# Other SBUF places for the moving operands of a two-layer diffusion backbone, and a DMA scratch of 1 KB

## The chip, the cores and the metric

The kernel runs on one core of a Trainium2 chip. The metric is the device time of one execution in microseconds (us). Before the change the median of three runs is 2012.92 us (2012.64 to 2014.09).

## The reference

Two layers run over 256 latent tokens `x` and 256 context tokens `ctx`, each of width 1024, with the same weights for both. All of it is float32. Cut to what matters:

```python
for l in range(DEPTH):                                   # DEPTH = 2
    m, mc = silu(c) @ w_ada[l] + b_ada[l], silu(c_ctx) @ w_ada[l] + b_ada[l]     # 9 x 1024 each
    x  = x  + 0.5 * m[2]  * swiglu(modulate(rms_norm(x),  m[0],  m[1]),  w1[l,0], w3[l,0], w2[l,0])
    xc = xc + 0.5 * mc[2] * swiglu(modulate(rms_norm(xc), mc[0], mc[1]), w1[l,0], w3[l,0], w2[l,0])
    h, hc = modulate(rms_norm(x), m[3], m[4]), modulate(rms_norm(xc), mc[3], mc[4])
    y, yc = token_mixer(h, hc, w_in[l], ...)             # yc only in layer 0
    x = x + m[5] * y
    x = x + 0.5 * m[8] * swiglu(modulate(rms_norm(x), m[6], m[7]), w1[l,1], w3[l,1], w2[l,1])
    # layer 0 alone: xc likewise
return rms_norm(x, final_g)
def swiglu(h, w1, w3, w2): return (silu(h @ w1) * (h @ w3)) @ w2      # 1024 -> 2816 -> 1024
def token_mixer(h, hc, w_in, ...):
    p = h @ w_in              # one projection: Fourier, retention, attention, gate logits
    f, r, d = fourier(p), retention(p, hc @ w_in), attention(p, hc @ w_in)
    return (g0 * (f @ w_branch_f) + g1 * (r @ w_branch_r) + g2 * (d @ w_branch_d)) @ w_out
```

## The kernel before

Activations stand transposed, channels on the 128 partitions and tokens along the free axis: 512 columns while both streams live, and 256 in the second half of layer 1, where only the latent tokens are left. Every large product is made of three float32r matmuls per 128x128 block of weights (`mm3`, L276 to L282): the weight is cut into a high part `whi` (a cast by ScalarE, L285) and a rest `wlo` (VectorE or, for a few, GpSimd, L286), the activation into `hi` and `lo` in the same manner, and L280, L281 and L282 add whi·hi, whi·lo and wlo·hi in PSUM. TensorE thus loads a new 128x128 weight tile before each matmul, and the activation is the moving operand that streams past it.

Weights come by DMA in pieces of [128, 4, 256] float32 into `wraw` (pool `wr`, four buffers), and the cut pieces stand in `whi` and `wlo` (pool `wh`, four buffers). The last quarter of each `to_residual` has its weights in the pool of its stage instead (tags "a", "b", "c" or "v").

The stages follow one another, named after layer and half: f00 (`ffn(0, 0)`, 512 columns), m0 (`mixer(0)`, 512), f01 and f10 (512), m1 (`mixer(1)`, 256 but for a few products over all 512 tokens), f11 (256). In an FFN the products into `p1`, `p3` read `hhi_f..`/`hlo_f..` (made by `Norm.parts`, L340), and the products into `py` read `ghi`/`glo` (the gated hidden units). In a mixer the products into `pj` (projections) and `pg` (gates) read `hhi_m..`/`hlo_m..`, those into `pb` (branches) `bh`/`bl`, and those into `py` (output) `mhi`/`mlo`. Two products of a mixer (`proj_tok`, L800) work the other way round: there a slice of `hhi_m..` is loaded as the weight, and 384 columns of `whi`/`wlo` move. At the seams between stages (`handover`, L456) the last products of one stage and the first of the next run for 256 columns at a time, and the first products of f11 read `xh`/`xl`, 258 columns wide.

Attention and retention are generators woven with the projections and gates (`weave`, L238), so that TensorE has products to run while VectorE and ScalarE work on masks and softmax. The order on each engine is fixed when the program is built.

Where a tile lies is set by the order in which the pools and their tiles are opened: each pool lays its tiles one after another at the next free byte of a partition. `hhi` and `hlo` have one place each in the pool `hp` for the whole kernel (L331 to L333); the tiles of an FFN lie in a pool opened at L578, those of a mixer in the pools opened at L722, L727, L728 and L1074. A pool named `shift` with one tile of 32 bytes stands ahead of them (L92).

The lines of the products:

```python
def mm3(o, wt, k, c0, x, start, stop):
    hi, lo = wt
    xh, xl = x
    a, b = hi[:, k, c0:c0 + P], lo[:, k, c0:c0 + P]
    te.matmul(o, a, xh, start=start, stop=False)
    te.matmul(o, a, xl, start=False, stop=False)
    te.matmul(o, b, xh, start=False, stop=stop)
```

Of the kernel before, what the change touches and what calls it, by code (L numbers as in the profile page):

```python
# [11 lines left out]
F32 = mybir.dt.float32  # L12
F32R = mybir.dt.float32r
# [4 lines left out]
P = 128  # L18
D = 1024
KD = D // P  # L20
L = 256
NTOK = 2 * L
# [57 lines left out]
def dit_kernel(ctx: ExitStack, tc: tile.TileContext, I: dict, out: bass.AP):  # L80
    nc = tc.nc
# [4 lines left out]
    hp = ctx.enter_context(tc.tile_pool(name="hp", bufs=1))  # L86
# [7 lines left out]
    def psum(name):  # L94
        return ps.tile([P, 2, 512], F32, tag="ps", name=name)

    def psum_bg(name):
        return ps.tile([P, 2, 512], F32, tag="psf", name=name)
# [63 lines left out]
    def modulated(l, m):  # L162

        if m % 3 == 1:
            n = m // 3
            v.scalar_tensor_tensor(amod[l][:, n], modT[l][:, m], 1.0, ng[:, l, n].unsqueeze(2).to_broadcast([P, KD, 2]),
                                   op0=ALU.add, op1=ALU.mult)
        if m in (2, 5, 8):
            v.tensor_scalar_mul(gmod[l][:, (2, 8, 5).index(m)], modT[l][:, m], 0.5)
# [30 lines left out]
    def ada(l, m, pool):  # L200

        acc = pool.tile([P, 2, D], F32, tag="aacc", name="aacc")
        for k in range(KD):
            w = wr.tile([P, D], F32, tag="wr", name="wada")
            sy.dma_start(w, I["w_ada"][l, k * P:(k + 1) * P, m * D:(m + 1) * D])
            for t in range(2):
                if k == 0:
                    v.tensor_scalar_mul(acc[:, t], w, cs[:, k, t:t + 1])
                else:
                    v.scalar_tensor_tensor(acc[:, t], w, cs[:, k, t:t + 1], acc[:, t], op0=ALU.mult, op1=ALU.add)  # L210
            yield
        pa = psum_bg(f"pa{l}_{m}")
        for q in range(4):
            te.matmul(pa[32 * q:32 * q + 32, 0, :], ones32, acc[:, q % 2, (q // 2) * 512:(q // 2 + 1) * 512],
                      start=True, stop=True, tile_position=(0, 32 * q))
        mrow = pool.tile([P, 512], F32, tag="mrow", name="mrow")
        v.tensor_copy(mrow, pa[:, 0, :])
        for b in range(4):
            te.transpose(pa[:, 1, b * P:(b + 1) * P], mrow[:, b * P:(b + 1) * P], ident)
        v.tensor_tensor(modT[l][:, m].rearrange("p (h b) t -> p h b t", h=2),  # L220
                        pa[:, 1, :].rearrange("p (b h t r) -> p h b t r", b=4, h=2, t=2)[:, :, :, :, 0],
                        biasT[l][:, 8 * m:8 * m + 8].rearrange("p (h b) -> p h b", h=2).unsqueeze(3)
                        .to_broadcast([P, 2, 4, 2]), ALU.add)
        modulated(l, m)
        yield
# [4 lines left out]
    def background(n):  # L230
        while n > 0 and pending:
            try:
                next(pending[0])
                n -= 1
            except StopIteration:
                pending.pop(0)
# [47 lines left out]
    def split_act(hi, lo, src, eng=v):  # L284
        s.copy(hi, src)  # L285
        eng.tensor_tensor(lo, src, hi.bitcast(F32), ALU.subtract)  # L286
# [38 lines left out]
    class Norm:  # L325

        def __init__(self, name, l, n, nt):
            self.name, self.l, self.n, self.nt = name, l, n, nt
            self.raw = {}

        def places(self):  # L331
            self.hi = hp.tile([P, KD, NTOK], F32R, tag="hhi", name=f"hhi_{self.name}")
            self.lo = hp.tile([P, KD, NTOK], F32R, tag="hlo", name=f"hlo_{self.name}")  # L333

        def scale(self, st, t, k):
            c = slice(t * L, (t + 1) * L)
# [29 lines left out]
    class Entry(Norm):  # L366
# [37 lines left out]
        def product(self, t, k):  # L404
            c = slice(t * L, (t + 1) * L)
            hi, lo = self.hi, self.lo
            if self.early:
                c, hi, lo = slice(0, L + 2), self.xh, self.xl
            if not self.accs:
                self.accs = [get(name) for get, name, _ in self.gets]  # L410
            for acc, chunks, (_, _, tiles) in zip(self.accs, self.chunks, self.gets):
                wt, k0, _ = chunks[k // 4]
                for m in range(tiles):
                    mm3(acc[:, m, c], wt, k - k0, m * P, (hi[:, k, c], lo[:, k, c]), k == 0, k == KD - 1)
# [108 lines left out]
    def load(w, kt, c0, r0=0, pool=None, tags=()):  # L523

        return [(split([rowsof(w, r0 + k, min(4, kt - k), c0, 2 * P)], min(4, kt - k), 2 * P,
                       pool and (pool, tags[k // 4])), k, min(4, kt - k))
                for k in range(0, kt, 4)]
# [44 lines left out]
    def ffn(l, f, nt, norm, mods, then):  # L572


        hhi, hlo = norm.hi, norm.lo
        w1, w3, w2 = I["ffn_w1"][l, f], I["ffn_w3"][l, f], I["ffn_w2"][l, f]
        st = Stats(f"f{l}{f}")
        with tc.tile_pool(name=f"ffn{l}{f}", bufs=1) as fp:  # L578
            steps = (ada(*m, fp) for m in mods)
            pending[:] = [x for x in steps]  # L580
            total = len(mods) * (KD + 1)
            state = [0, 0]

            def tick():
                state[0] += 1
                want = min(total, -(-total * state[0] // 56))
                with norm.done():
                    background(want - state[1])
                state[1] = max(want, state[1])

            for half, (g0, g1) in enumerate(((0, 6), (6, 11))):
                nk = 2 * (g1 - g0)
                ghi = fp.tile([P, 12, NTOK], F32R, tag="ghi", name="ghi")
                glo = fp.tile([P, 12, NTOK], F32R, tag="glo", name="glo")
                for g in range(g0, g1):
                    p1, p3 = norm.accs if g == 0 else (psum("p1"), psum_bg("p3"))
                    if g > 0:
                        for acc, w in ((p1, w1), (p3, w3)):
                            product(acc, load(w, KD, g * 2 * P), (hhi, hlo), nt)
                            tick()  # L600
                            tick()
                    j = slice(2 * (g - g0), 2 * (g - g0) + 2)
                    gt = fp.tile([P, 2, NTOK], F32, tag="gt", name="gt")[:, :, 0:nt]
                    if g == 0 and norm.early:
                        norm.gated(gt)
                    else:
                        s.activation(gt, p1[:, :, 0:nt], AF.Silu)
                        v.tensor_tensor(gt, gt, p3[:, :, 0:nt], ALU.mult)
                    split_act(ghi[:, j, 0:nt], glo[:, j, 0:nt], gt)
                for _ in to_residual(w2, nk, (ghi, glo), nt, gmod[l][:, f], st if half else None, fp, ("a", "b", "c"), 2 * g0,  # L610
                                     then):
                    tick()
        return st
# [72 lines left out]
    def mixer(l, nq, entry, then):  # L686

        nt = NTOK
# [3 lines left out]
        hhi, hlo = entry.hi, entry.lo  # L692
        win = I["w_in"][l]
        st = Stats(f"m{l}")
        shared = nq > L
# [24 lines left out]
            yield  # L720

        with tc.tile_pool(name=f"mx{l}", bufs=1) as mp:  # L722
            br = [mp.tile([P, n, nq], F32, name=f"br{i}_{l}") for i, n in enumerate((2, 3, 3))]

            mixed = [None, mp.tile([P, 4, nq], F32, name=f"mixB{l}") if shared else X[0][:, 0:4, L:NTOK]]
# [431 lines left out]
    after = start()  # L1157
    entry = mixer_entry(0)
    ffn(0, 0, NTOK, after, [(0, m) for m in range(2, 8)], entry)
    load_mixer_consts()  # L1160
    with after.done():
        for l in range(DEPTH):
            mixer_scalars(l)
    after = ffn_entry(0, 1, NTOK)
    mixer(0, NTOK, entry, after)
    load_bias(1)()
    entry = ffn_entry(1, 0, NTOK)
    ffn(0, 1, NTOK, after, [(0, 8)] + [(1, m) for m in range(4)], entry)
    after = mixer_entry(1)
    ffn(1, 0, NTOK, entry, [(1, m) for m in range(4, 9)], after)  # L1170
    entry = ffn_entry(1, 1, L)
    mixer(1, L, after, entry)
    ffn(1, 1, L, entry, [], Output())

# [21 lines left out]
```

## Time and profile before

| | before |
|---|---|
| median of three runs | 2012.92 us |
| the profiled execution's own time | 2012.76 us |
| its span, first to last instruction | 2011.0 us |
| TensorE matmuls busy | 1981.5 us, 99% of the span |
| weight loads (PEld), beside the matmuls | 1685.1 us, 84% |
| VectorE (DVE) busy | 1330.9 us, 66% |
| ScalarE (ACT) busy | 836.3 us, 42% |
| read from HBM | 283.5 MB, 143 GB/s over the span |
[...]

A matmul's duration in the profile reaches from its start to its modelled end, and matmuls overlap: one of 512 columns is shown with some 390 ns, while the next starts long before. What a stream of matmuls costs is the distance from one start to the next, read in the view of instructions in order of time. That view prints starts to 0.01 us, so a stretch of some twenty matmuls gives the spacing to about half a nanosecond.

### The profile page before, as it was taken

The page shows a single profiled execution, that of the slowest core. Times are in us where ns is not written, and L with a number is a line of the kernel's source. Part 1 is how long each engine was busy: PE and PEld are TensorE (multiplying, and loading weights), DVE is VectorE, ACT ScalarE, POOL GpSimd, SP SyncE. Part 2 cuts the span into 40 slices and gives each one's busy share as a digit, 9 for nine tenths or more (in the row PEclk, how much of TensorE's full clock was granted, in tenths as well). Part 3 has the DMA queues.
Part 4 walks back from the last instruction along what each step waited for, and adds up shares of the span by engine and source line. Part 5 has one row for each costly group of instructions (what it writes and reads, how often), then busy time and mean ns, then how long its engine had stood idle before and what let it go on. Part 6 is the DMA issues. An engine that isn't in the chain of part 4 may idle for free.

```text
span 2011.0 us, 27970 instructions
## 1 busy us (share of the span) xinstructions
PE 1981.5 (99%) x11087; PEld 1685.1 (84%) x11087; DVE 1330.9 (66%) x2038; ACT 836.3 (42%) x1286; POOL 51.7 (3%) x32
## 2 busy tenths in 40 slices
PE   7999999999999999999999999999999998999998
PEld 5887788898777788988788798877888988899998
DVE  6876666476588655765666566664665679877555
ACT  4432222365476534422122243221323758666443
POOL 2000000000001110000000000000000001110000
PEclk8999999999999999999999999999999999999999
DMA  9655555422213324354555425554553224465663
GB/s 298 217 178 173 172 172 173 115 97 83 77 53 97 118 89 123 120 160 146 176 168 157 134 69 189 178 156 125 166 168 105 64 88 143 145 196 162 187 185 115
DMA packets 240507, 288.47 MB, mean 143 GB/s; under 512 B 14368, under 2 KB 222328, under 8 KB 240120
## 3 DMA queue, kind: packets, MB, share of 16 engines
q1 hardware_dynamic: 240376, 286.69, 46.3%
q8 instruction: 87, 1.43, 0.3%
q14 instruction: 44, 0.36, 0.1%
HBM read 283.50 MB, written 3.15 MB: 143 GB/s over the span
## 4 chain that ended last, share of the span: by engine, by line
PE 92%; DVE 3%; ACT 2%; DMA 2%; issue 1%; POOL 0%; SPq 0%; DVEq 0%; ACTq 0%; POOLq 0%
PE p L280 14%; PE p L281 14%; PE p L282 14%; PE py L280 8%; PE py L281 8%; PE py L282 8%; PE pg L282 3%; PE pg L281 3%; PE pg L280 3%; PE pj L281 2%; PE pj L280 2%; PE pj L282 2%; PE pv L809 1%; PE pv L810 1%; PE pv L811 1%; DMA wada<-w_ada 1%
## 5 line engine op out<-in xcount | busy, mean ns | idle before, releaser
L285 ACT CAST whi<-wraw 128x1024 fp32r<-128x1024 f32 (+2 forms) x408 | 406.4, 1000 | 943.6 <-PE p L281 417.0
L286 DVE TENSOR_TENSOR wlo<-wraw,whi 128x1024 fp32r<-128x1024 f32 (+2 forms) x380 | 445.0, 1177 | 348.4 <-ACT whi L285 347.4
L280 PE MATMUL p<-hhi_f,whi 128*128 128x512 f32 (+1 forms) x1440 | 516.1, 359 | 0.4 <-DVE hhi_f L352 0.4
L282 PE MATMUL p<-hhi_f,wlo 128*128 128x512 f32 (+1 forms) x1440 | 513.3, 356 | 1.1 <-POOL wlo L286 0.6
L281 PE MATMUL p<-hlo_f,whi 128*128 128x512 f32 (+1 forms) x1440 | 513.9, 357 | 0.2
L280 PEld LDWEIGHTS p<-hhi_f,whi 128*128 128x128 f32 x1440 | 272.3, 189 | 48.3 <-ACT whi L285 5.9
L282 PEld LDWEIGHTS p<-hhi_f,wlo 128*128 128x128 f32 x1440 | 272.3, 189 | 41.1 <-POOL wlo L286 1.3
L210 DVE SCALAR_TENSOR_TENSOR aacc<-wada,cs,aacc 128x1024 f32<-128x1024 f32 x224 | 277.3, 1279 | 42.6 <-DMA wada<-w_ada 42.3
L281 PEld LDWEIGHTS p<-hlo_f,whi 128*128 128x128 f32 x1440 | 272.3, 189 | 38.8 <-DVE hlo_f L357 1.0
L280 PE MATMUL py<-ghi,whi 128*128 128x512 f32 (+1 forms) x764 | 269.0, 352 | 0.0
L281 PE MATMUL py<-glo,whi 128*128 128x512 f32 (+1 forms) x764 | 267.6, 350 | 0.0
L282 PE MATMUL py<-ghi,wlo 128*128 128x512 f32 (+1 forms) x764 | 267.5, 350 | 0.0
L280 PEld LDWEIGHTS py<-ghi,whi 128*128 128x128 f32 x764 | 143.9, 188 | 26.1 <-issue 4.2
L282 PEld LDWEIGHTS py<-ghi,wlo 128*128 128x128 f32 x764 | 143.9, 188 | 21.3
L281 PEld LDWEIGHTS py<-glo,whi 128*128 128x128 f32 x764 | 143.9, 188 | 21.0
L280 PE MATMUL pg<-hhi_m,whi 128*128 128x512 f32 (+1 forms) x384 | 132.5, 345 | 0.0
L282 PE MATMUL pg<-hhi_m,wlo 128*128 128x512 f32 (+1 forms) x384 | 130.6, 340 | 1.3 <-DVE wlo L286 1.2
L281 PE MATMUL pg<-hlo_m,whi 128*128 128x512 f32 (+1 forms) x384 | 130.3, 339 | 0.0
L286 POOL TENSOR_TENSOR wlo<-wraw,whi 128x768 fp32r<-128x768 f32 (+2 forms) x28 | 51.5, 1842 | 1732.0 <-ACT whi L285 1675.0
L507 DVE SCALAR_TENSOR_TENSOR xT<-py,gmod,xT 128x256 f32<-128x256 f32 x136 | 59.1, 478 | 54.5 <-PE py L282 54.2
L280 PE MATMUL pj<-hhi_m,whi 128*128 128x256 f32 (+1 forms) x288 | 92.9, 323 | 0.0
L281 PE MATMUL pj<-hlo_m,whi 128*128 128x256 f32 (+1 forms) x288 | 92.7, 322 | 0.2
(270 smaller groups left out, 2525.0 us busy)
## 6 DMA issues: line engine op xcount, KB each, us to landing
wraw<-ffn_w SPq DMA_DIRECT2D x256, 512.0 KB, 3.8
wada<-w_ada SPq DMA_DIRECT2D x128, 512.0 KB, 3.8
wraw<-w_in SPq DMA_DIRECT2D x64, 512.0 KB, 3.6
wada<-w_ada SPq DMA_DIRECT2D x32, 256.0 KB, 6.8
wraw<-w_out SPq DMA_DIRECT2D x16, 512.0 KB, 3.4
wraw<-w_in SPq DMA_DIRECT2D x16, 384.0 KB, 3.4
wraw<-w_in SPq DMA_DIRECT2D x20, 256.0 KB, 3.0
wraw<-ffn_w SPq DMA_DIRECT2D x16, 256.0 KB, 2.7
```

The costliest lines, as they stand in the source:

```text
L210: v.scalar_tensor_tensor(acc[:, t], w, cs[:, k, t:t + 1], acc[:, t], op0=ALU.mult, op1=ALU.add)
L280: te.matmul(o, a, xh, start=start, stop=False)
L281: te.matmul(o, a, xl, start=False, stop=False)
L282: te.matmul(o, b, xh, start=False, stop=stop)
L285: s.copy(hi, src)
L286: eng.tensor_tensor(lo, src, hi.bitcast(F32), ALU.subtract)
L507: v.scalar_tensor_tensor(X[0][:, d, c], acc, gate[:, d, t:t + 1], X[0][:, d, c], op0=ALU.mult, op1=ALU.add)
L809: te.matmul(o, hhi[:, kk, ts], hi[:, k], start=(kk == 0), stop=False)
L810: te.matmul(o, hhi[:, kk, ts], lo[:, k], start=False, stop=False)
L811: te.matmul(o, hlo[:, kk, ts], hi[:, k], start=False, stop=(kk == KD - 1))
```

## The change

The change gives some tiles another place in SBUF and does no more: it has no instruction that was not there before, and on each of the five engines the instructions and their waits stand in the same order, row for row.

- `hhi` and `hlo` get 256 elements more than they need. For m1 and f11 the part in use begins 48 elements, 192 bytes, further on; for the other stages it begins at the start.
- In an FFN `ghi` and `glo` are now the first tiles of their pool. With 512 columns a pad of 208 floats (832 bytes, which is 320 modulo 512) stands ahead of them, and in every FFN such a pad stands behind them, ahead of the other tiles of the pool.
- In m0 a pad of 208 floats is the first tile of the mixer's pool.
- The scratch that the program sets aside in SBUF for DMA descriptors shrinks from 16384 to 1024 bytes. All tiles move down by the difference, 15360 bytes, which is 30 times 512; the place modulo 512 stays.

```diff
             self.raw = {}
 
+            self.shift = 48 if name in ("m1", "f11") else 0
+
         def places(self):
-            self.hi = hp.tile([P, KD, NTOK], F32R, tag="hhi", name=f"hhi_{self.name}")
-            self.lo = hp.tile([P, KD, NTOK], F32R, tag="hlo", name=f"hlo_{self.name}")
+            self.hi, self.lo = (hp.tile([P, KD * NTOK + 256], F32R, tag=x, name=f"{x}_{self.name}")
+                                [:, self.shift:self.shift + KD * NTOK].rearrange("p (k n) -> p k n", k=KD)
+                                for x in ("hhi", "hlo"))
...
         with tc.tile_pool(name=f"ffn{l}{f}", bufs=1) as fp:
+            if nt == NTOK:
+                fp.tile([P, 208], F32, name="pad0")
+            for x in ("ghi", "glo"):
+                fp.tile([P, 12, NTOK], F32R, tag=x, name=x)
+            fp.tile([P, 208], F32, name="pad1")
...
         with tc.tile_pool(name=f"mx{l}", bufs=1) as mp:
+            if shared:
+                mp.tile([P, 208], F32, name="pad")
...
-    nc = _bacc.Bacc("TRN2", target_bir_lowering=False, num_devices=1)
+    nc = _bacc.Bacc("TRN2", target_bir_lowering=False, num_devices=1, dynamic_dma_scratch_size=1024)
```

The two built programs give each tile's address. "Distance" below is the byte at which the moving operand of a matmul begins, less the byte at which its weights begin, modulo 512. Every block of a tile (`k`, `m`) begins a multiple of 512 bytes further on, so one number holds for a whole tile. In both programs the `whi`/`wlo` of the pool `wh` lie at 96 modulo 512; the moving tiles lie at 96 or at 288.

| moving tile, columns | matmuls | distance before | after |
|---|---|---|---|
| hhi/hlo of f00, m0, f01, f10, 512 | 3792 | 0 | 0 |
| ghi/glo of f00, f01, f10, 512 | 1404 | 192 | 0 |
| bh/bl of m0, 512 | 192 | 192 | 0 |
| mhi/mlo of m0, 512 | 144 | 192 | 0 |
| hhi/hlo of m1, 512 (dk projections) | 48 | 0 | 192 |
| hhi/hlo of f11, 256 | 960 | 0 | 192 |
| hhi/hlo of m1, 256 | 960 | 0 | 192 |
| ghi/glo, last quarter of w2, weights in the stage's pool, 256 | 420 (60 of them in f11) | 0 | 192 |
| ghi/glo of f11, the rest, 256 | 468 | 192 | 192 |
| bh/bl and mhi/mlo of m1 with weights in `wh`, 256 | 336 | 192 | 192 |
| hhi/hlo at the entries of m0, f01, f10, and mhi/mlo with weights in the stage's pool, 256 | 720 | 0 | 0 |
| whi/wlo past hhi/hlo of m0, 384 | 192 | 0 | 0 |
| whi/wlo past hhi/hlo of m1, 384 | 192 | 0 | 320 |

## Rows read from the trace of the kernel before

**Rows 1.** The page: busy time of each engine, share of the span, instructions.
```profile
PE 1981.5 (99%) x11087; PEld 1685.1 (84%) x11087; DVE 1330.9 (66%) x2038; ACT 836.3 (42%) x1286; POOL 51.7 (3%) x32
```
**Rows 2.** The page: the chain that ended last, by engine and by line.
```profile
PE 92%; DVE 3%; ACT 2%; DMA 2%; issue 1%; POOL 0%; SPq 0%; DVEq 0%; ACTq 0%; POOLq 0%
```
**Rows 3.** Groups by line and shape, PE: line, tiles, shape, count | busy us, mean ns.
```profile
L280 PE MATMUL py<-ghi,whi 128*128 128x512 f32 x468 | 185.8, 397 | 0.0
...
L280 PE MATMUL py<-ghi,whi 128*128 128x256 f32 x296 | 83.2, 281 | 0.0
...
L280 PE MATMUL pb<-bh,whi 128*128 128x512 f32 x64 | 25.4, 397 | 0.0
```
**Rows 4.** PE in order of time, f01, into p: start us, us, instruction (21 spacings).
```profile
900.03 0.39 PE L280 MATMUL p<-hhi_f,whi 128*128 128x512 f32 x1
...
904.79 0.39 PE L280 MATMUL p<-hhi_f,whi 128*128 128x512 f32 x1
```
**Rows 5.** The same view, f01, into py (26 spacings).
```profile
999.72 0.40 PE L280 MATMUL py<-ghi,whi 128*128 128x512 f32 x1
...
1005.78 0.40 PE L282 MATMUL py<-ghi,wlo 128*128 128x512 f32 x1
```
**Rows 6.** The same view, f11, into p (35 spacings).
```profile
1849.77 0.28 PE L280 MATMUL p<-hhi_f,whi 128*128 128x256 f32 x1
...
1853.97 0.28 PE L282 MATMUL p<-hhi_f,wlo 128*128 128x256 f32 x1
```
**Rows 7.** The same view, f11, into py, where the last quarter begins (24 and 11 spacings).
```profile
1991.91 0.28 PE L280 MATMUL py<-ghi,whi 128*128 128x256 f32 x1
...
1994.63 0.28 PE L280 MATMUL py<-ghi,whi 128*128 128x256 f32 x1
1994.75 0.28 PE L281 MATMUL py<-glo,whi 128*128 128x256 f32 x1
...
1995.95 0.28 PE L282 MATMUL py<-ghi,wlo 128*128 128x256 f32 x1
```
**Rows 8.** The same view, m1, proj_tok, 384 columns (18 spacings).
```profile
1609.82 0.33 PE L809 MATMUL pv<-whi,hhi_m 128*128 128x384 f32 x1
...
1612.94 0.33 PE L809 MATMUL pv<-whi,hhi_m 128*128 128x384 f32 x1
```
**Rows 9.** The same view, entry of f11, 258 columns (20 spacings).
```profile
1822.82 0.28 PE L280 MATMUL p<-xh,whi 128*128 128x258 f32 x1
...
1825.21 0.29 PE L282 MATMUL p<-xh,wlo 128*128 128x258 f32 x1
```
**Rows 10.** Busy time by stretch: attention of m1; f01; f11's first 144 us.
```profile
1660.00:1735.00 75.00, 67.55 (x505) 62.21 (x503) 69.77 (x134) 60.19 (x118) 10.99 (x7) 1.00 0.45 143
...
797.00:1172.00 375.00, 374.48 (x1802) 308.73 (x1802) 233.63 (x277) 113.65 (x143) 0.00 (x0) 1.00 0.49 149
1836.00:1980.00 144.00, 144.00 (x1221) 144.00 (x1220) 79.51 (x81) 63.34 (x72) 0.00 (x0) 1.00 0.62 188
```
**Rows 11.** The same view, pg alone, the attention of m1 (PE, PEld, ACT).
```profile
1660.00:1690.00 30.00, 14.01 (x98) 12.74 (x98) 1.31 (x4) 1.00 0.43 136
1690.00:1720.00 30.00, 17.46 (x133) 16.41 (x134) 1.31 (x4) 1.00 0.50 158
1720.00:1735.00 15.00, 10.32 (x80) 9.62 (x78) 1.30 (x4) 1.00 0.41 126
```
**Rows 12.** Who PE waited for in that stretch: us in total, times, longest.
```profile
PE po L886 <- DVE osq L291: 1.3, 1, 1.3
PE pg L282 <- DVE wlo L286: 1.2, 2, 1.0
```
**Rows 13.** The page: DMA queues: packets, MB, share of 16 engines' span.
```profile
q1 hardware_dynamic: 240376, 286.69, 46.3%
q8 instruction: 87, 1.43, 0.3%
q14 instruction: 44, 0.36, 0.1%
```

## The prediction

> **What bounds the kernel now.** I read the page's busy times first, then the chain of waits, then TensorE's groups by line and shape, and then single stretches of TensorE in order of time. TensorE is busy 1981.5 of 2011.0 us, VectorE 66% and ScalarE 42% [rows 1], and 92% of the chain that ended last is TensorE's own instructions [rows 2]. So the time is the number of matmuls times the spacing of their starts, and all but about 30 us of the span is that. An edit that changes the spacing shows in the time directly; one on another engine shows only where TensorE stands still.
>
> The spacing is not one number for one shape. In f01 the products of hhi_f, 512 columns at distance 0, start 4.76 us / 21 = 226.7 ns apart [rows 4]. The products of ghi and glo, as wide, with weights cut in the same manner, but at distance 192, start 6.06 / 26 = 233.1 ns apart [rows 5]. With 256 columns the order is the other way round. In f11 hhi_f at distance 0 has 4.20 / 35 = 120.0 ns [rows 6]. The rows that decide most are of one tile: while ghi and glo meet weights of the pool wh, distance 192, they start 2.72 / 24 = 113.3 ns apart; from 1994.63 us, when the last quarter's weights come from the stage's own pool and the distance is 0, the spacing is 1.32 / 11 = 120.0 ns [rows 7]. Tile, shape, engine load and instruction are the same on both sides of that moment; only the place of the weights differs. So the place of the moving tile alone does not decide, nor its pool. For 512 columns no tile is seen at both distances, so there the pool is not excluded in this manner. [...]
>
> TensorE stands still for any length of time in one place beside start and end: in the attention of m1 it is busy 67.55 of 75 us, VectorE 69.77 [rows 10], and it waits for VectorE's and ScalarE's results a microsecond at a time [rows 12].
>
> **The change part by part.** The sum is made against the profiled execution's own 2012.76 us (a span of 2011.0 and 1.76 around it), which lies 0.16 us under the median of the three runs; I let the two stand for each other. No instruction is added, removed or moved, and no wait. What changes is the distance.
>
> *512 columns from 192 to 0.* The ghi/glo products are 468 per line on three lines [rows 3], 1404; with bh/bl (64 per line, 192) and mhi/mlo (144) that is 1740 matmuls. Each goes from 233.1 to 226.7 ns [rows 4, 5]: 1740 x 6.4 ns = 11.1 us off. They run in f00, m0, f01 and f10, where TensorE is hardly ever without work (374.48 of 375 us in f01 [rows 10]) and where the weights are cut ahead (VectorE 233.63 of 375), so all of it is on the path.
>
> *512 columns from 0 to 192.* The 48 dk projections of m1 lose 48 x 6.4 ns = 0.3 us.
>
> *256 columns from 0 to 192.* hhi/hlo of f11 (960), hhi/hlo of m1 (960) and the ghi/glo of the last quarters (420 of the 888 that the 296 per line make [rows 3]) are 2340 matmuls. Each goes from 120.0 to 113.3 ns [rows 6, 7]: 2340 x 6.7 ns = 15.7 us off. In f11 TensorE is busy 144.00 of 144 us while VectorE has 79.51 and ScalarE 63.34 [rows 10], so its 1020 matmuls count in full, and a supply of weights that is asked for 6% faster is far from late.
>
> *What the attention of m1 takes back.* Of the pg products at 256 columns, 98 + 133 + 80 = 311 lie between 1660 and 1735 us [rows 11]. Their 311 x 6.7 ns = 2.1 us shorten a stretch in which VectorE is busy 93% of the time. Where TensorE next waits for VectorE or ScalarE, it only waits longer; where its own products stand last, it gains. The bounds are 0 and 2.1 us lost; TensorE is busy 90% there and VectorE 93%, so neither is clearly last, and I take the middle, 1.0 us lost.
>
> *384 columns from 0 to 320.* In proj_tok of m1 the 192 matmuls have 173.3 ns at distance 0 [rows 8], and no row shows this width or this distance elsewhere. The nearest rows bound it: 6.4 ns more (what 192 costs at 512 columns) or 6.7 ns less (what it gives at 256), so 1.2 us lost to 1.3 us gained. The width lies halfway between the two, and I take 0.
>
> *Everything else.* The 336 and 468 matmuls of 256 columns that are at 192 stay there; those at the seams of the 512-column stages stay at 0. The smaller DMA scratch moves all tiles by a multiple of 512 and so leaves every distance as it is. All 240376 data packets run on the one hardware queue, the other two queues bring instructions [rows 13], so I cost it at nothing; were I wrong, it would show as later weights at the very start. The writes of ScalarE and VectorE into moved tiles could lengthen or shorten; these engines are not on the path outside the attention, and I take 0.
>
> Sum: 11.1 - 0.3 + 15.7 - 1.0 = 25.5 us, and 2012.76 - 25.5 = 1987.3 us.
>
> [...]
>
> **The rivals.**
> *No change, 2012.8 us.* The spacing belongs to something that goes along with the distance in these rows, such as which pool the weights come from: both steps of [rows 7] and the slow ghi of [rows 5] would then stay. For it: at 258 columns, with distances between 192 and 312, the spacing is 2.39 / 20 = 119.5 ns [rows 9], not 113.3, so 192 and its neighbours are no cure for every width. Against it: weights of the same pool wh go with 120.0 ns in [rows 6] and with 113.3 ns in [rows 7]. 4%. [...]
>
> *Only the 256-column part, 2012.8 - 15.7 + 1.0 + 0.3 = 1998.4 us.* At 512 columns ghi, bh and mhi could be slow for another reason than the distance, since no tile is seen both ways. Against it: three tiles of different pools and makers share the 233 ns, and what the hhi of four stages share is the distance 0. 5%.
>
> *Attention becomes the bound and turns the sign, over 2012.8 us.* VectorE has 75 - 69.77 = 5.2 us to spare in the 75 us of attention [rows 10]. If the new places slowed its instructions there, TensorE would wait for all that goes beyond 5.2 us; to eat the 25.5 us, VectorE's work would have to grow by 30.7 us, 44%. From 44% on the kernel is slower than before; at 60% it would lose 41.9 - 5.2 = 36.7 us there and end at 2012.8 + 36.7 - 25.5 = 2024 us. For it: VectorE is nearly full there. Against it: the moved tiles are hardly among its operands, and elsewhere it would have to grow by over half before it counted (233.63 of 375 us). 2%.
>
> **How the numbers follow.** The forecast, all widths by distance, has 89% and 1987.3 us. Its own bounds are 26.5 + 1.3 = 27.8 us off at best (nothing lost in attention, 384 columns faster) and 26.5 - 2.1 - 1.2 = 23.2 us off at worst: 1985.0 to 1989.6 us. The spacings are read to half a nanosecond, which on 4080 matmuls is 2 us to either side; and disturbed spacings, where an operand waits anyway, may keep a little of the gain. The range is 1983.5 to 1993, which leaves out the 1998.4 of the second rival and the two others. A measurement of this kernel can tell about 0.2%, 4 us, from no change: the forecast and the 256-column case are faster, 94%; no change has 4%, slower 2%.
>
> **What would show it right or wrong.** In the profile after: ghi in f01 start some 227 ns apart instead of 233; hhi_f in f11 some 113 instead of 120, and no step at the start of the last quarter of f11; f01 and f10 are each 3 to 4 us shorter and f11 near 7 us; the attention of m1 is between 0 and 2.1 us shorter, with longer waits; the dk projections of m1 start 233 ns apart; proj_tok of m1 says what 384 columns do at 320. Wrong would be: spacings that stay, spacings that move to other values than these four, or a VectorE that is busy longer.

## The result, and the profile after

The changed kernel takes 1999.81 us (median of four runs, 1994.98 to 2003.08) against 2013.15 before. The ratio is 0.9931, with a 95% interval of 0.9911 to 0.9952: it is faster, by 13 us where 25.5 were forecast, and the time lies outside the range of 1983.5 to 1993. The four runs lie 8 us apart; those of before lie 1.5 us apart. The profiled execution has 2003.08 us and a span of 2001.3, and what follows is read against that.

From the page after, the busy times and the chain that ended last (they answer to [rows 1] and [rows 2]):
```profile
PE 1970.8 (98%) x11087; PEld 1684.3 (84%) x11087; DVE 1331.5 (67%) x2038; ACT 836.5 (42%) x1286; POOL 52.2 (3%) x32
...
PE 91%; DVE 4%; ACT 2%; DMA 2%; issue 1%; POOL 0%; SPq 0%; DVEq 0%; ACTq 0%; POOLq 0%
```
TensorE still sets the time, and the busy time of every other engine is within 1 us of before. So the missing 12 us must be in TensorE's spacings, its waits or its clock.

TensorE of the kernel after in order of time (start us, us, instruction), first the ghi and glo products of f01, 27 spacings:
```profile
999.74 0.39 PE L281 MATMUL py<-glo,whi 128*128 128x512 f32 x1
...
1005.86 0.39 PE L281 MATMUL py<-glo,whi 128*128 128x512 f32 x1
```
6.12 / 27 = 226.7 ns, where [rows 5] had 233.1: the 512-column part came out as forecast. Now hhi_f in f11, 36 spacings:
```profile
1839.74 0.28 PE L282 MATMUL p<-hhi_f,wlo 128*128 128x256 f32 x1
...
1843.98 0.28 PE L282 MATMUL p<-hhi_f,wlo 128*128 128x256 f32 x1
```
4.24 / 36 = 117.8 ns, neither the 120.0 of [rows 6] nor the 113.3 of [rows 7]. And it is not hhi_f alone: the ghi products of f11, which had 113.3 before and whose distance did not change, have 117.8 now as well. From 8.6 us after the first hhi_f product on, f11 stands at 117.8 ns; ahead of that it has stretches at 113.3 (lines under lock11 below).

In m1, first the dk projections (13 spacings), then proj_tok, whose width no row showed at another distance (18):
```profile
1608.56 0.40 PE L282 MATMUL pj<-hhi_m,wlo 128*128 128x512 f32 x1
...
1611.59 0.39 PE L280 MATMUL pj<-hhi_m,whi 128*128 128x512 f32 x1
```
```profile
1599.82 0.34 PE L819 MATMUL pv<-whi,hhi_m 128*128 128x384 f32 x1
...
1602.94 0.34 PE L819 MATMUL pv<-whi,hhi_m 128*128 128x384 f32 x1
```
3.03 / 13 = 233.1 and 3.12 / 18 = 173.3 ns: both as taken.

The attention of m1 holds something else. After, busy time by stretch (PE, PEld, DVE, ACT, POOL, then the granted clock and DMA):
```profile
1650.00:1690.00 40.00, 35.29 (x253) 31.72 (x251) 37.51 (x81) 36.72 (x70) 4.14 (x4) 1.00 0.41 132
1690.00:1697.00 7.00, 5.72 (x33) 5.52 (x34) 6.83 (x11) 3.52 (x10) 1.02 (x1) 0.76 0.43 136
1697.00:1725.00 28.00, 26.41 (x216) 24.32 (x215) 25.30 (x42) 19.23 (x39) 6.18 (x3) 1.00 0.51 155
1725.00:1731.00 6.00, 5.44 (x33) 4.86 (x35) 4.04 (x13) 4.43 (x9) 0.00 (x0) 0.72 0.30 90
```
In two places the granted clock falls to 0.50 for part of the stretch, from 1692.8 us and from 1726.9 us on, for 3.4 us each. TensorE in order of time around the second:
```profile
1723.28 0.28 PE L282 MATMUL pg<-hhi_m,wlo 128*128 128x256 f32 x1
1725.56 0.66 PE L994 MATMUL pT<-k_ident,ex 128*128 128x128 f32 x4 [2.00 <-ACT ex L981]
...
1727.23 0.42 PE L280 MATMUL pb<-bh,whi 128*128 128x256 f32 x1
...
1729.59 0.41 PE L282 MATMUL pb<-bh,wlo 128*128 128x256 f32 x1
```
TensorE stands 2.00 us, waiting for ScalarE; soon after it has work again, its products start 2.36 / 11 = 214.5 ns apart instead of 113 or 118, and then the clock returns. The same wait before was 1.55 us, and in the profile of before the granted clock is 1.00 all through m1.

Stage by stage, in us. The first row ends at the first product of m1, the second at m1's first gate product, the third at m1's last product. The row f11 runs from its first hhi_f product to TensorE's last product; the products of `xh`/`xl` between the last two rows take the same 12.5 us in all three profiles. lock11 is an experiment below.

| stage | forecast | before | after | lock11 |
|---|---|---|---|---|
| f00, m0, f01, f10 | -13.5 | 1532.38 | 1522.03 | - |
| m1, projections and retention | -2.3 | 110.38 | 109.93 | 109.17 |
| m1, gates, attention, branches | -2.9 | 143.59 | 144.46 | 142.72 |
| f11 | -6.8 | 178.97 | 178.88 | 173.26 |

The first row gave 10.4 us. m1 and f11, from which 12.0 us were forecast, together gave nothing in this execution.

### The profile page after: what moved, and what is told of

It reads as the page before. It is cut to its first block, busy times and chain, and to the rows that moved or that the text cites. A ratio compares the mean times of both kernels' runs of the same rounds, so it can differ in the third digit from the quotient of the medians.

```text
span 2001.3 us, 27970 instructions
## 1 busy us (share of the span) xinstructions
PE 1970.8 (98%) x11087; PEld 1684.3 (84%) x11087; DVE 1331.5 (67%) x2038; ACT 836.5 (42%) x1286; POOL 52.2 (3%) x32
## 4 chain that ended last, share of the span: by engine, by line
PE 91%; DVE 4%; ACT 2%; DMA 2%; issue 1%; POOL 0%; SPq 0%; DVEq 0%; ACTq 0%; POOLq 0%
PE p L280 14%; PE p L282 14%; PE p L281 14%; PE py L280 8%; PE py L282 8%; PE py L281 8%; PE pg L282 3%; PE pg L281 3%; PE pg L280 3%; PE pj L281 2%; PE pj L280 2%; PE pj L282 2%; PE pv L819 1%; PE pv L821 1%; PE pv L820 1%
```

## The experiments

Theory 1, formed from the profile after: a stream of 256-column products at distance 192 has two steady spacings, 113.3 and 117.8 ns, and what ran before it picks one. In the profile of before, the stretches at 113.3 ns in f11 and m1 came after products at distance 0. The rival (theory 2): the spacing at 192 is one number and something else on the chip slows f11.

**sweep.** A kernel of its own: streams at each distance from 0 to 480 in steps of 32.
```python
for d in range(0, 512, 32):
    stream(o[:, 0], 256, 0, 12); stream(o[:, 1], 256, d, 40)      # 12 products at 0, then 40 at d
    for q in range(6):
        upset(z[:, 0])                                            # three float32 products, then one of
        te.matmul(z[:, 1, 0:128 + 24 * q], whi[:, 7], flat[:, 0:128 + 24 * q], start=True, stop=True)
        stream(o[:, q % 2], 256, d, 40)
```


> A kernel of its own: streams of 40 float32r matmuls of 256 columns (24 of 384 and 512) past weights that lie 0, 32, ... 480 bytes before them modulo 512, each stream once right after a stream at distance 0 and several times after short float32 products and one matmul of 128 to 248 columns. It computes none of the reference's result. Theory 1 (a stream of 256 columns at distance 192 has two steady spacings, and what runs just before it picks one): at 192 some streams settle at 113.3 ns and some at 117.8 ns, and those that follow distance 0 directly at 113.3; at 0 all have 120.0. Theory 2 (the spacing at 192 is one number, 113.3 ns, and f11 was slowed by something else on the chip): every stream at 192 settles at 113.3 ns. For 512 columns both expect 226.7 at 0 and 233 at 192; 384 columns at 320: 173.3.

The streams of 384 and 512 columns, whose code is not shown here, run the same way, 24 products each, one straight after distance 0 and one after `upset`. The settled spacing, the mean of the last twelve spacings of a stream, in ns:

| distance | 0 | 32 | 64 | 96 | 128 | 160 | 192 | 224 |
|---|---|---|---|---|---|---|---|---|
| 256 columns | 120.0 | 116.7 or 117.8 | 117.8 | 120.0 | 118.4 to 118.9 | 117.1 to 119.0 | **113.3 or 117.8** | 118.2 to 118.8 |
| 384 columns | 173.3 | 173.3 | 173.3 | 176.7 | 175.8 to 176.4 | 173.3 or 176.7 | 173.3 or 176.7 | 173.3 |
| 512 columns | 226.7 | 233.3 | 228.9 | 233.3 | 232.9 or 233.3 | 234.2 or 234.6 | 233.3 | 233.3 |

Distances from 256 on repeat the row to within 0.2 ns, so what counts in these streams is the distance modulo 256, not 512. At 192 three of the seven streams settled at 117.8 ns, the one straight after distance 0 at 113.3. Theory 1 holds, and theory 2 falls. Two values at one place are not special to 256 columns: 384 columns have 173.3 or 176.7 at 160 and at 192. For 512 columns 0 is the best of the distances tried.

**only512.** The moves of the 512-column products alone.
```diff
-            self.shift = 48 if name in ("m1", "f11") else 0
+            self.shift = 0
...
-            for x in ("ghi", "glo"):
-                fp.tile([P, 12, NTOK], F32R, tag=x, name=x)
-            fp.tile([P, 208], F32, name="pad1")
+                for x in ("ghi", "glo"):
+                    fp.tile([P, 12, NTOK], F32R, tag=x, name=x)
```


> The moved tiles of the 512-column products alone (ghi/glo, bh/bl, mhi/mlo to distance 0); the 256-column products keep the distances of before. Both theories: 1740 matmuls x 6.4 ns = 11.1 us off, 2002 us, and runs that differ by less than 2 us, as those of before do.

Measured: 2002.19 us (2001.81 to 2003.35), ratio 0.9945 (0.993 to 0.9959), 11.2 us under the 2013.34 of before in that batch. f00, m0, f01 and f10 are 11.0 us shorter. The term is right, and it is steady. Its m1, with the spacings of before, also had a half clock once, so such a fall does not need the change.

**only256.** The moves of the 256-column products alone.
```diff
-            if nt == NTOK:
-                fp.tile([P, 208], F32, name="pad0")
...
-            if shared:
-                mp.tile([P, 208], F32, name="pad")
```


> The 256-column products alone are moved to 192; the 512-column ones keep the distances of before. Theory 1: between nothing and 13 us off, 2000 to 2013 us, with runs that differ from each other by over 3 us, since f11 can settle at 113.3 or at 117.8 ns, 1428 matmuls x 4.4 ns = 6.3 us apart. Theory 2: one time, 2012 us, with runs within 2 us.

Measured: 2010.63 us, ratio 0.9976 (0.9965 to 0.9987); the ten runs fall in two groups, seven from 2009.60 to 2011.54 and three from 2002.68 to 2005.00. They are 5 to 9 us apart; f11 at 113.3 or 117.8 ns makes 1488 x 4.5 ns = 6.7 us. The profiled one had 117.8 ns in f11, but for its first 9 us, and is of the longer group.

**again.** The changed kernel, not edited.

> The changed kernel once more, nothing edited. Theory 1: runs spread over 5 us or more between 1994 and 2004, and the f11 of the profiled run stands at 113.3 or 117.8 ns for long stretches, not necessarily as in the first profile. Theory 2: f11 stands at 117.8 again.

Measured: 1999.68 us, runs from 1996.44 to 2003.36, f11 at 117.8 ns in the profiled one, which is the longest. The spread belongs to the kernel; that the shorter runs have 113.3 is inferred, since no profile shows one of them.

**lock11 and ctl11.** Six products more in f11, ahead of g == 2; in lock11 at distance 0, in ctl11 at 192.
```diff
+        for k in range(more):                             # lock11: 6 where nt == L and g == 2, for w1
+            te.matmul(acc[:, 0, 0:nt], chunks[0][0][0][:, 0, 0:P], chunks[0][0][0][:, k % 4, 0:nt], start=True, stop=True)
...
+            te.matmul(acc[:, 0, 0:nt], chunks[0][0][0][:, 0, 0:P], x[1][:, k, 0:nt], start=True, stop=True)     # ctl11
```


> The changed kernel with six more matmuls of 256 columns at distance 0 in f11, ahead of the products of g == 2 (they write an accumulator that the product then starts anew, so the result is the same). Theory 1 (two steady spacings at 192, picked by what runs before): after them f11 stands at 113.3 ns up to its last product in every run; about 1240 matmuls x 4.4 ns = 5.5 us less than where f11 stands at 117.8, plus 0.7 us for the six: 1995 to 1999 us with runs within 3 us. Rival (f11's 117.8 is what its load on the chip allows, and short runs are chance): 117.8 stays, 2000 us, and runs spread as for the changed kernel.

> The control: the same six matmuls in the same place and order, but with hlo as the moving operand, at distance 192. Theory 1: they pick nothing; f11 goes on as it was, at 117.8 in most runs, 1995 to 2004 us as the changed kernel plus 0.7 us. If six more matmuls of any kind put the stream right, f11 stands at 113.3 here too, 1995 to 1999 us.

Measured: lock11 1994.55 us (1993.36 to 1994.91), ratio 0.9906 (0.9889 to 0.9922); ctl11 1995.41 us (1994.38 to 1996.07). Busy time of the same 134 us of f11, first lock11, then the changed kernel run again:
```profile
1836.00:1970.00 134.00, 134.00 (x1184) 134.00 (x1184) 76.70 (x82) 61.61 (x71) 0.00 (x0) 1.00 0.63 191
```
```profile
1836.00:1970.00 134.00, 134.00 (x1140) 134.00 (x1139) 72.72 (x74) 57.62 (x65) 0.00 (x0) 1.00 0.61 184
```
1184 products against 1140 in one and the same time: 113.3 against 117.8 ns. But the control stands at 113.3 too, against what was expected of it, and in both profiles f11 was there before the six came. So the pair does not tell whether they do anything. Nor does it show that they shorten the kernel: both ran on another chip than again, without the changed kernel beside them.

Where f11 takes its lasting spacing can be read in both. First the changed kernel, then lock11, whose six begin at 1825.12 us:
```profile
1821.83 0.28 PE L280 MATMUL p<-hhi_f,whi 128*128 128x256 f32 x1
...
1824.10 0.38 PE L281 MATMUL p<-hlo_f,whi 128*128 128x256 f32 x1
1824.31 0.29 PE L282 MATMUL p<-hhi_f,wlo 128*128 128x256 f32 x1
...
1825.96 0.28 PE L282 MATMUL p<-hhi_f,wlo 128*128 128x256 f32 x1
```
```profile
1818.89 0.28 PE L280 MATMUL p<-hhi_f,whi 128*128 128x256 f32 x1
...
1821.15 0.37 PE L281 MATMUL p<-hlo_f,whi 128*128 128x256 f32 x1
1821.36 0.28 PE L282 MATMUL p<-hhi_f,wlo 128*128 128x256 f32 x1
...
1822.06 0.28 PE L282 MATMUL p<-hhi_f,wlo 128*128 128x256 f32 x1
...
1825.01 0.28 PE L282 MATMUL p<-hhi_f,wlo 128*128 128x256 f32 x1
```
Both stand at 113 ns (2.27 / 20 and 2.26 / 20) up to one longer spacing of 0.21 us, and behind it one goes on at 1.65 / 14 = 117.9 ns and the other, after a few products, at 2.95 / 26 = 113.5. All nine profiles with hhi_f of f11 at 192 have a longer spacing at this place, 0.125 to 0.22 us, 8.5 to 8.6 us after the first hhi_f product. Behind it f11 stands at 117.8 in after, again, only256 and late11, and at 113.3 in lock11, ctl11, latectl11 and the two variants of lock11 below. So it is at this short break of the stream, not at the entry into f11, that the two kinds of execution part; why it goes one way or the other is open.

**late11 and latectl11.** The same two insertions ahead of g == 7, a little over half way through f11 (`g == 7` in place of `g == 2`).

> The changed kernel with the six matmuls at distance 0 later in f11, ahead of the products of g == 7, after half of f11. Theory 1: where f11 entered at 117.8, the profile shows 117.8 up to them and 113.3 behind them; runs between 1994 and 2000 us, since up to 3 us are kept from being lost. Rival (how f11 is entered decides, and the six change nothing): one spacing from entry to end, and runs up to 2004.

> The control of the former: the six at distance 192 ahead of g == 7. Theory 1: the spacing of the entry goes on behind them, runs of 1994 to 2004 us. If any six matmuls do, 117.8 turns into 113.3 behind them here too.

Measured: late11 1997.57 us (1996.92 to 1998.90), latectl11 1995.45 us with runs of 1994.91, 1995.15, 1995.75 and 2002.20. TensorE of late11 in order of time:
```profile
1911.76 0.28 PE L281 MATMUL p<-hlo_f,whi 128*128 128x256 f32 x1
...
1915.30 0.28 PE L281 MATMUL p<-hlo_f,whi 128*128 128x256 f32 x1
...
1915.53 0.88 PE L517 MATMUL p<-whi 128*128 128x256 f32 x6
...
1916.60 0.28 PE L280 MATMUL p<-hhi_f,whi 128*128 128x256 f32 x1
...
1920.68 0.28 PE L280 MATMUL p<-hhi_f,whi 128*128 128x256 f32 x1
```
Ahead of the six 3.54 / 30 = 118.0 ns (117.8 from 1821 us on), behind them 4.08 / 36 = 113.3 ns, up to the last product of f11. The granted clock is 1.00 on both sides, and after, again and only256, which stand at 117.8 too and have nothing inserted, keep it past this point to the end of f11; six products at distance 0 changed it. The control already stood at 113.3 in its profile, so it could not show a change; its run of 2002.20 shows that six at 192 do not hold every execution at the shorter time.

**nudge.** A kernel of its own, at distance 192: a stream of 40, one of seven insertions, a stream of 40, six times each.
```python
if kind in (1, 2):          # six products with one weight tile, at distance 0 (1) or 192 (2)
if kind == 3:               # six at distance 0 with changing weights;  4: one at 0;  6: two at 0
if kind == 5:               # one product of 512 columns at distance 0;  0: nothing
```


> A kernel of its own, of 256-column products at distance 192 alone; it computes none of the reference's result. 42 times: short float32 products and one matmul of 128 to 248 columns, then 40 products, then one of seven insertions, then 40 products. In the sweep three of the six lengths left the stream at 117.8 ns. Theory 1 as first put: nothing inserted (kind 0) and six matmuls at 192 (kind 2) leave the spacing as it was; six at distance 0 with one weight tile or several (kinds 1 and 3), two (kind 6) or one at 0 (kind 4) or one of 512 columns (kind 5) bring every stream to 113.3. Rival (any break in the order of the weights does it): kinds 1 to 6 all bring it to 113.3.

| inserted | at 117.8 before: now 113.3 | at 113.3 before: now 117.8 |
|---|---|---|
| nothing (0) | 0 of 3 | 0 of 3 |
| six at 0, one weight tile (1) | 4 of 4 | 0 of 2 |
| six at 192 (2) | 0 of 3 | 0 of 3 |
| six at 0, changing weights (3) | 4 of 4 | 0 of 2 |
| one at 0 (4) | 1 of 4 | 0 of 2 |
| one of 512 columns (5) | - | 6 of 6 |
| two at 0 (6) | - | 6 of 6 |

In order of time, kind 1 and then kind 2 with the same stream ahead (x40 is one stream):
```profile
128.88 4.91 PE L36 MATMUL o<-mov,whi 128*128 128x256 f32 x40
133.62 0.88 PE L46 MATMUL o<-mov,whi 128*128 128x256 f32 x6
134.34 4.71 PE L36 MATMUL o<-mov,whi 128*128 128x256 f32 x40
...
193.02 4.91 PE L36 MATMUL o<-mov,whi 128*128 128x256 f32 x40
197.77 0.87 PE L46 MATMUL o<-mov,whi 128*128 128x256 f32 x6
198.48 4.87 PE L36 MATMUL o<-mov,whi 128*128 128x256 f32 x40
203.19 0.83 PE L40 MATMUL z<-ident 128*128 128x128 f32 x6
```
After six at 0 the second stream takes 4.71 us instead of 4.91; after six at 192 it takes 4.87, as the first. The rival, any break, falls; so does the part of theory 1 that one or two products at 0 would do, or one of 512. Two at 0, or one of 512, put every stream here from 113.3 to 117.8; one at 0 brought one of four to 113.3 and left the rest as they were. Undisturbed (kind 0), all six streams kept their spacing.

**lock11_m1old.** lock11 with hhi/hlo of m1 back at distance 0.
```diff
-            self.shift = 48 if name in ("m1", "f11") else 0
+            self.shift = 48 if name == "f11" else 0
```


> As with the six matmuls at distance 0 in f11, but hhi/hlo of m1 back at distance 0, so that the moved m1 is left out. Theory 1 with m1's gain lost to VectorE, to 117.8 and to a halved clock: within 1.5 us of the kernel with m1 moved, its m1 254 us, its f11 172 us. Rival (m1's 256-column products gain 6.7 ns each as forecast, and only f11 failed): 5 us slower than the kernel with m1 moved.

Measured: 1996.38 us (1995.40 to 1997.13), 1.8 us more than lock11; m1 takes 254.1 us (110.38 and 143.70) where lock11 has 251.9. The rival falls. Theory 1's 1.5 us was a little low: against lock11, moving m1 is worth 2 us, not the 5.2 of the forecast.

**lock11_fill.** lock11 with 16 products ahead of the transposes that TensorE waited for.
```diff
+                                    for q in range(16 if n == 7 else 0):
+                                        te.matmul(pT[:, 0, 0:L], hhi[:, 0, 0:P], hlo[:, q % 8, 0:L], start=True, stop=True)
```


> As with the six matmuls at distance 0 in f11, and 16 matmuls of 256 columns (1.9 us) ahead of the transposes in m1's attention for which TensorE waited 2.2 us with nothing to do. Their product is overwritten. Theory (the clock is halved for 3.4 us right after that wait because TensorE stood still): the stretch at half clock after it is gone from the trace and 1 to 2 us come off. Rival (the half clock has nothing to do with the wait): it stays, and the time is the same or longer by part of the 1.9 us.

Measured: 1995.65 us (1994.97 to 1996.38), 1.1 us more than lock11. No fall of the clock in m1, but lock11 itself had none either in its profile (granted clock 1.00 from 1650 to 1740 us), so this run decides nothing on the cause. Nor did the 16 fill the wait: TensorE still stands 2.01 us waiting for ScalarE, and the 16 run behind that wait, ahead of the transposes. The gate part of m1 takes 144.49 us instead of 142.72, about what 16 products cost; the edit also moved some instructions of ScalarE and VectorE there.

## Why the prediction was wrong

**512 columns, right.** 226.7 ns, 11.1 us forecast, 11.2 us measured by only512. The rival that put the 233 ns down to the tiles falls: with nothing moved but the start of the moving operand, the sweep has 226.7 ns at distance 0 and 233.3 at 192. Why the place has a price no run shows.

**256 columns, the step that failed.** "Each goes from 120.0 to 113.3 ns" took one of two values for the price of the distance. At 192 there are two, and the rows of before showed only one, because the stretch in [rows 7] followed products at distance 0 in f11; in nudge six such products gave 113.3 in 8 of 8 cases. The change took these away: it put everything in f11 at 192, and so nothing behind its first microseconds brings the short spacing back once a break has ended it. In the profiled execution f11 stood at 117.8 ns: 1020 products won 2.2 ns each and the 468 that had 113.3 before lost 4.5, 2.2 us against 2.1, together nothing. The ghi products at the seams of the 512-column stages also went to about 117.8, 0.7 us where 2.4 were forecast. The argument "only the place of the weights differs" on [rows 7] showed that the place has a price, but not that 113.3 is the only value at 192: it was the value after products at distance 0. And the row at 258 columns [rows 9], told as a rival's, was a hint that there are more than the two values. The first row of the stage table, 10.4 us, is 1.3 us under the 11.0 of only512 and these 0.7 together; the same stages gave 10.8 us in again and 12.0 in late11, so single executions differ by as much.

**The attention of m1, mis-sized.** Of 5.2 us forecast for m1, after gave none and lock11 2.1. The mean spacing of m1's 256-column products ahead of the gates (starts under 0.2 us apart) went from 119.8 ns to 115.8 (after) and 114.2 (lock11), not to 113.3: behind each break by other products a stretch stands at 113.3 or at 117.8. In the gate part TensorE's waits grow from 7.9 us to 9.3 in lock11, counted as what the spacings over 330 ns have above 300: 1.4 us lost, where I took 1.0 and bounded by 2.1. What no step had is the clock: after has two stretches at a granted clock of 0.50 there, 3.4 us each, and 144.46 us, lock11 with the same places has none and 142.72. Compared product by product with lock11, after is 1.5 us late behind the first of them and makes up all but 0.2 us of it at the waits that follow, as latectl11 does, which has this one alone and 142.79 us. Behind the second it is 1.6 us later, and that stays. again has the second alone, 1.6 us, and 1.5 us more because its last gate, branch and output products stand at 117.8 ns where lock11 has 113.3: 145.81 us. Such falls also come without the moved m1 (only512 has one), and lock11, ctl11 and late11 have none. In the trace after, one follows a wait of 2.00 us; but ctl11 has the same wait, 2.00 us, and no fall, so the wait alone does not cause it, and the cause is open.

**384 columns, dk projections, scratch: as taken.** 173.3 and 233.1 ns, and no later start (4.8 us to the first transposes, 4.9 before). No run changes the scratch alone.

**The VectorE rival fell:** VectorE is busy 1331.5 us against 1330.9.

**The range** was too narrow mainly for one reason: 113.3 ns was given no error of its own but half a nanosecond. With 117.8 as the other bound, 2340 x 4.5 ns = 10.5 us above the forecast, it would have reached 1998 us, and 2000 with the 468 ghi products that lost theirs. Of the rest up to the 2003.08 us of the profiled execution, m1's clock has some 1.7 us.

## What to carry to other kernels

Where products follow each other without a pause, read the spacing of the starts, by width and by the distance between the moving operand and the weights modulo 256; here that is worth 3 to 6% of a matmul (226.7 against 233.3 ns at 512 columns, 113.3 against 120.0 at 256). A spacing seen in one stretch is the price of a place only when it is seen there after different pasts, so disturb it before you multiply it by a thousand. When runs of one kernel suddenly lie 8 us apart, look for a stream that can settle in two ways and put ahead of it what picks the better one. In nudge six products at distance 0 (0.7 us) did that for 8 of 8 streams, in late11 once in the kernel. The times of lock11 are no measure of it, since there f11 already stood at 113.3 when the six came.

## What the runs showed of the hardware that was not expected

- Two steady spacings of one and the same stream, 113.3 and 117.8 ns (256 columns, distance 192 or 448), each lasting over a thousand products; six products at distance 0 give the short one (8 of 8 that were at 117.8), one of 512 columns or two at distance 0 the long one (6 of 6 each that were at 113.3).
- The spacing repeats with a distance of 256 bytes; at 512 columns it is 226.7 ns at 0 and 228.9 to 234.6 at the other steps of 32 bytes.
- All nine profiles with f11's hhi_f at 192 have stretches at 113.3 ns in its first 8 us; behind one longer spacing 8.5 to 8.6 us in, four go on at 117.8 and five at 113.3. What decides, and why all four runs of ctl11 were short, is not settled.
- Falls of the granted clock in m1's attention (to 0.50, for 3.4 us, both times in after) come in some executions and not in others. Each puts TensorE 1.4 to 1.6 us behind; at one place the next waits made up all but 0.1 to 0.2 us of it, at the other none.
